# Where the y splits, one weight split and the last three p stand at the end of an attention

## The chip, the cores and the metric

The kernel runs on one core of a Trainium2 chip. The metric is device time in microseconds (us) of one execution. The core's engines run side by side, each through its own queue in program order: TensorE (PE in the profile; PEld are its weight loads), VectorE (DVE), ScalarE (ACT), GpSimd (POOL), and SyncE (SP), which here only issues DMAs. An instruction that waits holds up everything behind it on its engine.

## The reference, cut to what matters

One encoder layer for 1024 tokens and 1024 channels: a modulated RMS norm, one input projection, a pooling branch (512 channels) beside an attention with 8 heads (512 channels), an output projection and a gated residual.

```python
u_pool, g_pool, q_lat, kv_lat, k_rope_raw, g_attn = jnp.split(proj, offs, axis=-1)
y_pool = multiscale_pool(u_pool, pool_w[l], pool_scale[l]) * jax.nn.silu(g_pool)
...
s = jnp.einsum('bqhd,bkhd->bhqk', qblk, k, preferred_element_type=jnp.float32) * scale
p = jax.nn.softmax(s, axis=-1)
return jnp.einsum('bhqk,bkhd->bqhd', p.astype(v.dtype), v)
...
y = jnp.einsum('bsm,md->bsd', jnp.concatenate([y_pool, y_attn], axis=-1), w_out[l])
h = h + gate[:, None, :] * y
```

## The kernel before, in words

Products keep float32 accuracy by splitting each operand in two: a rounded **high half** and a **low half**, the rest (x minus high). Three matmuls, high·high, high·low and low·high, are summed. For the attention the halves are float16, for the projections a rounded float32.

**The attention** is a hand-written software pipeline (line 1005) over 64 jobs. Job i belongs to head i // 8 and step i % 8. Steps 0 to 3 (`hf` = 1) each take 128 query rows against all keys; steps 4 to 7 (`hf` = 0) each take 256 keys against the other 512 query rows. Tiles are named by head, `hf` and number: `st612` are the scores of head 6, `hf` 1, number 2, which is job 50; `st703` those of job 63. A job passes these stations:

- `scores`: six matmuls into a pair of PSUM banks (`st`). There are two such pairs in rotation; job 1 of each head (step 1) uses a third pair (tag `r`), which also holds the row maxima scores of `prep_max` and the transposed outputs `yt`. With `hf` = 1 DVE then takes the maximum over the row and scales it (L808, L809, tile `bp`).
- `expo` (ACT, L819): p = exp of the scores, into a tile `p` in SBUF, or in place, when `in_psum(i)` is true.
- `p_hi` (ACT, L824) and `p_lo` (L831): the two float16 halves of p (tile `ph`). `p_lo` runs on POOL, and on DVE for jobs whose p is in PSUM, which POOL doesn't read here. Before, those are steps 1 and 7 of a head, from job 7 on.
- `p_turn` (SP): with `hf` = 1 a DMA transposes `ph` to `pt`.
- `attend`: 16 matmuls into `av`, six jobs (LAG) behind `scores`; then `out_copy` (ACT L868, DVE L869) and `out_norm` (DVE L875, POOL L879) after the last job of a half head.

In steps 4 to 7 of head 6, `prep_max` takes the row maxima for four query blocks of head 7 (scores `rs70` to `rs73` on TensorE, maximum on DVE, L733). The maxima go into the first column of the tile `src1h` (the q source of the odd heads), and after the fourth a DMA transposes that column into q (L735).

**Work of the output projection that is put into the attention.** A table `extra`, filled by `at(head, step, ...)`, runs at the end of a step; steps 8 to 14 of head 7 are the seven in which the pipeline drains.

- `out_split` (L935 ACT, L937 POOL): the two halves of the output weights `oraw` of output tiles 0 and 1, in two pieces each, into `owhi` and `owlo`. For tile 1 these lie where `src1h` and its k counterpart were.
- `y_split` (L914 or L916 high half, L918 low half): the two halves of y0 to y6, the inputs of the output projection. y0 to y3 are the pooling outputs, y4 to y6 are heads 0 to 5, two heads each (tiles `gT0` to `gT2`; the last of them is ready after `out_tr` in step 4 of head 7). y7 (heads 6 and 7) follows behind the pipeline.
- `fill(0, k, k+1)`, steps 8 to 14: the six matmuls of y_k for output tile 0 (`ops`, L974). Behind the pipeline come tiles 1 to 7, 48 matmuls each.

What is on each engine in which order is thus set by the order of the calls within a step and by the two tables `XS`/`XS2` and `YP`.

Of the kernel before, what the change touches and what calls it, by code (L numbers as in the profile page):

```python
# [8 lines left out]
F32 = mybir.dt.float32  # L9
# [8 lines left out]
P = 128  # L18
# [3 lines left out]
H = 8  # L22
# [8 lines left out]
INV_2PI = 0.15915494309189535  # L31
INP = (1, 7)
XH = 6
XS = (4, 5)
XS2 = (2, 2)
YP = ((0, 4, 5, 1), (1, 6, 7, 1), (2, 8, 8, 1), (3, 9, 9, 0), (4, 10, 10, 0), (5, 11, 11, 0), (6, 12, 12, 0))
NF = 7
SG = 12
LAG = 6
# [19 lines left out]
def body(ctx, tc, small, cond, xT, ada_sc, ada_sh, ada_gt, w_lat, w_fm, pool_w, w_uq, w_ukv, gains, pos, w_out, out):  # L59
    nc = tc.nc  # L60
    V, A, G, T, SY = nc.vector, nc.scalar, nc.gpsimd, nc.tensor, nc.sync
# [146 lines left out]
    with ExitStack() as pa:  # L208
# [29 lines left out]
        for k in range(NK):  # L238
            pool, tag = (wp, "raw") if k in (0, 1, 6, 7) else (mp, wu_tags[k - 2])
# [462 lines left out]
    def conv_hi(h, w, eng, t0=0, t1=NK):  # L702
        o_, i_ = srcs[h % 2][w][:, 0, t0:t1, 1:HW], (QT, KT)[w][:, t0:t1, h, :]
        if eng is A:
            A.activation(o_, i_, AF.Copy)
        else:
            eng.tensor_copy(o_, i_)
# [40 lines left out]
    stp = ctx.enter_context(tc.tile_pool(name="psS", bufs=2, space=PSUM, reuse_waits="tile"))  # L748
    avp = ctx.enter_context(tc.tile_pool(name="psV", bufs=1, space=PSUM, reuse_waits="tile"))
    rsp = ctx.enter_context(tc.tile_pool(name="psR", bufs=1, space=PSUM, reuse_waits="tile"))  # L750
# [39 lines left out]
    def scores(i, n):  # L790
        h, hf, j = jobs[i]
        if n == 0:
            pool, tag = (rsp, "r") if h and hf and j == 1 else (stp, "st")
            stt[i] = pool.tile([P, 2, 512], F32, tag=tag, name=f"st{h}{hf}{j}")
        qh_, ql_ = qs[h]
        kh_, kl_ = ks[h]
        if hf == 0:
            kt = j * 2 + n
            for a, (l, r) in enumerate(((kh_, qh_), (kh_, ql_), (kl_, qh_))):
                T.matmul(stt[i][:, n], l[:HW, kt * P:(kt + 1) * P], r[:HW, 0:512], start=(a == 0), stop=(a == 2))  # L800
            return
        qt = 4 + j
        for a, (l, r) in enumerate(((qh_, kh_), (qh_, kl_), (ql_, kh_))):
            T.matmul(stt[i][:, n], l[:HW, qt * P:(qt + 1) * P], r[:HW, n * 512:(n + 1) * 512],  # L804
                     start=(a == 0), stop=(a == 2))
        if n:
            bps[i] = ep.tile([P, 1], F32, tag="bp", name=f"bp{h}{j}")
            V.tensor_reduce(bps[i], stt[i], AX.XY, ALU.max)  # L808
            V.tensor_scalar(bps[i], bps[i], nesc, 6.0 * LN2, ALU.mult, ALU.add)  # L809
# [15 lines left out]

    def in_psum(i):

        return i % 8 in INP and (i > 7 or i == 7)

    def p_lo(i):  # L830
        (V if in_psum(i) else G).tensor_tensor(pas[i][:, 1], pfs[i], pas[i][:, 0], ALU.subtract)  # L831
# [1 line left out]
    def p_turn(i):  # L833
        h, hf, j = jobs[i]
        if hf:
            pts[i] = a_tile("t", [P, 2 * NK, P], f"pt{h}{j}")
            SY.dma_start_transpose(pts[i], pas.pop(i).rearrange("p a n c -> p (a n c)"))
# [4 lines left out]
    def attend(i, n):  # L842
        h, hf, j = jobs[i]
        if j == 0 and n == 0:
            avt[0] = avp.tile([P, 2, 512], F32, tag="av", name=f"av{h}{hf}")

        def acc(qt, kt, hi, lo):
            o_ = avt[0][:, qt // 2, (qt % 2) * 256:(qt % 2) * 256 + 129]
            T.matmul(o_, hi, VT[:, kt, h, 0:129], start=kt == 0 and qt % 2 == 0, stop=False, skip_group_check=True)  # L849
            T.matmul(o_[:, 0:65], lo, VT[:, kt, h, 0:65], start=False, stop=kt == NK - 1, skip_group_check=True)  # L850

        if hf == 0:
            for qt in range(4):
                c_ = slice(qt * P, (qt + 1) * P)
                acc(qt, j * 2 + n, pas[i][:, 0, n, c_], pas[i][:, 1, n, c_])
            if n:
                pas.pop(i)
        else:
            for kt in range(4 * n, 4 * n + 4):
                acc(j, kt, pts[i][:, kt], pts[i][:, NK + kt])  # L860
# [3 lines left out]
    def out_copy(i):  # L864
        h, hf, _ = jobs[i]
        a4 = avt[0].rearrange("p b (i c) -> p (b i) c", i=2)
        ov = ovs[h, hf] = rb[:, hf * 512:hf * 512 + 260].rearrange("p (i c) -> p i c", i=4)
        A.activation(ov, a4[:, :, 64:129], AF.Copy)  # L868
        V.tensor_tensor(ov[:, :, 1:], a4[:, :, 0:64], ov[:, :, 1:], ALU.add)  # L869
# [14 lines left out]
    def out_tr(h, hfs, pt):  # L884
        for hf in hfs:
            for j in range(4):
                T.transpose(pt[:, hf, j * P:(j + 1) * P], opair[h // 2][:, hf, j, :], ident)
        c_ = slice(hfs[0] * 512, hfs[-1] * 512 + 512)
        pv = pt[:, hfs[0]:hfs[-1] + 1].rearrange("p b c -> p (b c)")
        if h < H - 1:  # L890
            V.scalar_tensor_tensor(gT[h // 2][:, c_], pv, vinv, gT[h // 2][:, c_], ALU.mult, ALU.mult)
        else:
            if not last:
                last.append(dp.tile([P, S], F32, tag="t0", name="ylast"))
            V.tensor_copy(last[0][:, c_], pv)
# [52 lines left out]
    def at(h, step, f, *a):  # L948
        extra.setdefault((h, step), []).append((f, a))
# [3 lines left out]
    for n in range(2):  # L953
        for part in range(2):
            for d in range(2):
                at(XH + d, XS[part] + XS2[d] * n, out_split, d, (n,), (part,), G)

    xr, ps = {}, {}

# [2 lines left out]
        SY.dma_start(xr[d], xT[d])  # L962

    def new(d):
        pool, tag = (stp, "st") if d % 3 < 2 else (rsp, "r")
        t_ = pool.tile([P, 2, 512], F32, tag=tag, name=f"ops{d}")
        ps[d] = [t_[:, 0], t_[:, 1]]

# [23 lines left out]
    at(7, 8, new, 0)  # L992
    for k in range(NF):
        at(7, 8 + k, fill, 0, k, k + 1)
    for k, s0, s1, e_ in YP:
        at(7, s0, y_split, k, (0, 1), (0,), (A, V)[e_])
        at(7, s1, y_split, k, (0, 1), (1,))

    def early(i, p_):

        for j in range(4):
            if RS0[j] == (i, p_):
                prep_max(0, j)

    for i in range(len(jobs) + LAG + 1):
        live = i < len(jobs)
        h, step = i // 8, i % 8
        a_ = i - LAG
        av_ok = 0 <= a_ < len(jobs)
        rh = h + (step > 3)  # L1010
        RSP = RSPY if rh in (4, 6, 8) else RSPN
        rsu = RSP.index(step) if live and 0 < rh < H and step in RSP else None
        e_ = i - 1 if 0 <= i - 1 < len(jobs) else None
        if 0 <= i - 3 < len(jobs):
            p_turn(i - 3)
        if av_ok and step in AF0:
            attend(a_, 0)
            attend(a_, 1)
            if jobs[a_][2] == 3:
                out_copy(a_)  # L1020
        early(i, 0)
        if live:
            scores(i, 0)
        early(i, 1)
        if live and h + 2 < H and step > 3:
            if step % 2 == 0:
                conv_hi(h + 2, 3 - step // 2, V)
            conv_lo(h + 2, 3 - step // 2, G, step % 2 * 4, step % 2 * 4 + 4)
        if live and 0 < h < H - 1 and step in TS:
            turn(h + 1, 1 - TS.index(step))  # L1030

        for hf in range(2):
            for n_ in (a_ - ON[hf],) if live else range(a_ - ON[hf], a_):
                if 0 <= n_ < len(jobs) and jobs[n_][1:] == (hf, 3) and jobs[n_][:2] in ovs:
                    out_norm(n_)
        if e_ is not None and jobs[e_][1] == 0:
            expo(e_)
        if 0 <= i - 2 < len(jobs):
            p_hi(i - 2)
            p_lo(i - 2)  # L1040
            pfs.pop(i - 2)
        if e_ is not None and jobs[e_][1]:
            expo(e_)
        if av_ok and step not in AF0 + AFL:
            attend(a_, 0)
        if NE + i < NK:
            last_fm(NE + i, NE + i + 1)
        if NE + i == NK - 1:
            last_end()
        early(i, 2)  # L1050
        if live:
            scores(i, 1)
        early(i, 3)
        if i == 3:
            fm_bias(11, lraw, rsp.tile([P, 2, 512], F32, tag="r", name="psb11")[:, 0])
        if av_ok and step in AFL:
            attend(a_, 0)
        if live and step == 4 and h in (3, 5, 7):
            out_tr(h - 2, (0, 1), rsp.tile([P, 2, 512], F32, tag="r", name=f"yt{h}"))
        if rsu is not None:  # L1060
            prep_max(rh, rsu)
        if av_ok and step not in AF0:
            attend(a_, 1)
            if jobs[a_][2] == 3:
                out_copy(a_)
        if i == 68:
            out_tr(H - 1, (1,), rsp.tile([P, 2, 512], F32, tag="r", name="yt8"))
        for f, a in extra.pop((min(h, H - 1), i - 8 * min(h, H - 1)), []):
            f(*a)
    assert not extra  # L1070
# [22 lines left out]
    for d in range(2, NK):  # L1093
# [15 lines left out]
        else:  # L1109
            for m, (a, b) in enumerate(LPARTS):  # L1110
                c_ = slice(a, b)
                pt = ps[d][0] if m == 0 else (rsp, avp)[m % 2].tile([P, 2, 512], F32, tag=("r", "av")[m % 2],
                                                                    name=f"opsl{m}")[:, 0]
# [80 lines left out]
```

## Time and profile before

| | |
|---|---|
| median of 3 runs | 501.46 us (501.36 to 502.86) |
| the execution profiled | 500.05 us, span of its trace 498.3 us |
| TensorE busy | 464.9 us, 93% of the span |
| DVE / ACT / POOL busy | 355.9 / 253.8 / 234.4 us |
| head 6, first scores of job 48 to those of job 56 | 354.18 to 374.79 us |
| head 7, from there to the scores of job 63 | 374.79 to 392.54 us |
| granted TensorE clock, mean of the span | 0.996 |

In the page's 40 slices of 12.5 us TensorE and its granted clock look like this (tenths, 9 is 90% or more); DVE and POOL beside them:

```profile
PE   5999998999999999999989888898898969999997
DVE  4888849999999853577677887877867985913221
POOL 1950040201242949448869796787869780000000
PEclk9999999999999999999999999999999999999999
```

The dip to 6 in slice 33 is the end of the attention (399 to 411 us). Timeline rows of the trace give the start from the span's start, the length, engine, line, operation and tiles, and in brackets how long the engine had been idle before and what ended that. Times are from one execution.

### The profile page before, as it was taken

The page shows a single profiled execution, that of the slowest core. Times are in us where ns is not written, and L with a number is a line of the kernel's source. Part 1 is how long each engine was busy: PE and PEld are TensorE (multiplying, and loading weights), DVE is VectorE, ACT ScalarE, POOL GpSimd, SP SyncE. Part 2 cuts the span into 40 slices and gives each one's busy share as a digit, 9 for nine tenths or more (in the row PEclk, how much of TensorE's full clock was granted, in tenths as well). Part 3 has the DMA queues.
Part 4 walks back from the last instruction along what each step waited for, and adds up shares of the span by engine and source line. Part 5 has one row for each costly group of instructions (what it writes and reads, how often), then busy time and mean ns, then how long its engine had stood idle before and what let it go on. Part 6 is the DMA issues. An engine that isn't in the chain of part 4 may idle for free.

```text
span 498.3 us, 7657 instructions
## 1 busy us (share of the span) xinstructions
PE 464.9 (93%) x2956; PEld 355.0 (71%) x2956; DVE 355.9 (71%) x565; ACT 253.8 (51%) x338; POOL 234.4 (47%) x190
## 2 busy tenths in 40 slices
PE   5999998999999999999989888898898969999997
PEld 3999876898888888785555555555555658888886
DVE  4888849999999853577677887877867985913221
ACT  3756038993203030226878888888899861001000
POOL 1950040201242949448869796787869780000000
PEclk9999999999999999999999999999999999999999
DMA  8894442000102110144786779779982836753333
GB/s 300 332 307 159 171 142 65 6 1 7 47 1 91 34 58 27 57 86 95 170 148 138 162 145 176 152 151 163 224 175 63 160 113 231 276 182 129 126 128 126
DMA packets 117046, 66.33 MB, mean 133 GB/s; under 512 B 105873, under 2 KB 107793, under 8 KB 117010
## 3 DMA queue, kind: packets, MB, share of 16 engines
q1 hardware_dynamic: 117010, 65.85, 49.9%
q8 instruction: 23, 0.38, 0.3%
q14 instruction: 13, 0.11, 0.1%
HBM read 35.43 MB, written 4.19 MB: 80 GB/s over the span
## 4 chain that ended last, share of the span: by engine, by line
PE 49%; DVE 22%; ACT 10%; POOL 10%; issue 5%; DMA 3%; SPq 0%; ACTq 0%; DVEq 0%; POOLq 0%
PE ops L974 14%; PE fps L170 8%; PE st L800 4%; PE pq L548 3%; ACT ph L824 3%; PE lps L234 3%; DVE bp L808 3%; POOL fraw L152 3%; ACT p L819 3%; DMA wlr<-in_w_lat 2%; PE rs L730 2%; PE av L849 2%; PE st L804 2%; POOL s L614 2%; DVE ph L831 2%
## 5 line engine op out<-in xcount | busy, mean ns | idle before, releaser
L831 POOL TENSOR_TENSOR ph<-p,ph 128x1024 f16<-128x1024 f32 x49 | 105.9, 2168 | 13.1 <-ACT ph L824 10.2
L170 PE MATMUL fps<-xh,whi 128*128 128x512 f32 x192 | 62.0, 404 | 0.5 <-ACT whi L147 0.5
L170 PE MATMUL fps<-xh,wlo 128*128 128x512 f32 x192 | 59.3, 390 | 0.1
L170 PE MATMUL fps<-xl,whi 128*128 128x512 f32 x192 | 59.3, 390 | 0.0
L800 PE MATMUL st<-q,k 97*128 97x512 f16 x192 | 49.5, 379 | 6.7 <-ACT p L819 6.6
L804 PE MATMUL st<-k,q 97*128 97x512 f16 x192 | 48.2, 379 | 8.0 <-ACT p L819 6.4
L824 ACT ACTIVATE ph<-p 128x1024 f16<-128x1024 f32 x49 | 51.7, 1055 | 0.5
L152 POOL TENSOR_TENSOR fraw<-fraw,shift 128x1024 f32<-128x1024 f32 x7 | 22.7, 3237 | 60.8 <-DVE wlo L148 53.8
L808 DVE TENSOR_REDUCE bp<-st 128x1 f32<-128x1024 f32 x32 | 39.0, 1220 | 5.2 <-PE st L804 3.4
L170 PEld LDWEIGHTS fps<-xh,whi 128*128 128x128 f32 x192 | 35.5, 189 | 9.0 <-ACT whi L147 1.0
L170 PEld LDWEIGHTS fps<-xh,wlo 128*128 128x128 f32 x192 | 36.0, 188 | 8.1 <-DVE wlo L148 0.5
L170 PEld LDWEIGHTS fps<-xl,whi 128*128 128x128 f32 x192 | 36.1, 188 | 7.7
L935 ACT ACTIVATE owhi<-oraw 128x1024 fp32r<-128x1024 f32 (+1 forms) x10 | 8.8, 885 | 54.0 <-DMA oraw<-in_w_out 54.0
L819 ACT ACTIVATE p<-st,bp,esc 128x1024 f32<-128x1024 f32 x25 | 30.1, 1204 | 9.4 <-DVE bp L809 9.0
L804 PEld LDWEIGHTS <-q 97*128 97x128 f16 x192 | 16.6, 97 | 25.6 <-issue 10.9
L800 PEld LDWEIGHTS <-k 97*128 97x128 f16 x192 | 16.6, 97 | 21.5 <-issue 8.3
L624 ACT ACTIVATE dh<-s 128x1024 fp32r<-128x1024 f32 x4 | 4.2, 1062 | 51.9 <-DVE s L621 51.9
L819 ACT ACTIVATE p<-st,ebias,esc 128x1024 f32<-128x1024 f32 x24 | 28.9, 1203 | 2.5 <-PE st L800 1.3
L850 PE MATMUL av<-VT,ph 128*128 128x65 f16 x256 | 26.4, 193 | 2.9 <-POOL ph L831 2.9
L849 PE MATMUL av<-VT,pt 128*128 128x129 f16 x256 | 28.0, 221 | 0.8 <-DMA pt<-ph 0.8
L849 PE MATMUL av<-VT,ph 128*128 128x129 f16 x256 | 27.7, 221 | 0.2 <-DVE rb L869 0.2
L850 PEld LDWEIGHTS <-ph 128*128 128x128 f16 x256 | 22.6, 98 | 7.1 <-POOL ph L831 3.1
(297 smaller groups left out, 1142.5 us busy)
## 6 DMA issues: line engine op xcount, KB each, us to landing
fraw<-in_w_fm SPq DMA_DIRECT2D x12, 512.0 KB, 3.7
asc<-in_ada_sc SPq DMA_DIRECT2D x8, 512.0 KB, 6.0
xr<-in_xT SPq DMA_DIRECT2D x8, 512.0 KB, 5.3
ash<-in_ada_sh SPq DMA_DIRECT2D x8, 512.0 KB, 6.8
oraw<-in_w_out SPq DMA_DIRECT2D x8, 512.0 KB, 5.1
xres<-in_xT SPq DMA_DIRECT2D x8, 512.0 KB, 5.0
agt<-in_ada_gt SPq DMA_DIRECT2D x8, 512.0 KB, 5.7
out_dram<-xres SPq DMA_DIRECT2D x7, 512.0 KB, 3.0
```

Of the source, the lines that this page charges most:

```text
L152: G.tensor_tensor(pb, pb, shift.unsqueeze(2).broadcast_to([P, NK, P]), ALU.mult)
L170: T.matmul(ps[n], w[:, k, :], x_[k][:, n * 512:(n + 1) * 512], start=(k == order[0] and j == 0), stop=(k == order[-1] and j == 2))
L234: T.matmul(ps[:, :LAT], l[k][:, ts_], r[k], start=(k == 0 and i == 0), stop=(k == NK - 1 and i == 2))
L800: T.matmul(stt[i][:, n], l[:HW, kt * P:(kt + 1) * P], r[:HW, 0:512], start=(a == 0), stop=(a == 2))
L804: T.matmul(stt[i][:, n], l[:HW, qt * P:(qt + 1) * P], r[:HW, n * 512:(n + 1) * 512], start=(a == 0), stop=(a == 2))
L808: V.tensor_reduce(bps[i], stt[i], AX.XY, ALU.max)
L819: A.activation(pfs[i], st, AF.Exp, bias=bps.pop(i) if hf else ebias, scale=esc)
L824: A.activation(pas[i][:, 0], pfs[i], AF.Copy)
L831: (V if in_psum(i) else G).tensor_tensor(pas[i][:, 1], pfs[i], pas[i][:, 0], ALU.subtract)
L849: T.matmul(o_, hi, VT[:, kt, h, 0:129], start=kt == 0 and qt % 2 == 0, stop=False, skip_group_check=True)
L850: T.matmul(o_[:, 0:65], lo, VT[:, kt, h, 0:65], start=False, stop=kt == NK - 1, skip_group_check=True)
L974: T.matmul(ps[d][n], w_[:, k, :], y_[k][:, n * 512:(n + 1) * 512], start=(k == 0 and j == 0), stop=(k == NK - 1 and j == 2))
```

## The change

Four tables or rules change. The y splits move from steps 4 to 12 of head 7 to head 6, step 1 to head 7, step 7, and all seven high halves are made by DVE (before, y3 to y6 by ACT). The split of output tile 1's weights moves from steps 4 to 7 of head 7 to its steps 0 to 3; that of tile 0 stays. The p of jobs 61 and 62 stays in PSUM beside that of job 63, and DVE, not POOL, makes their low halves. The PSUM tiles of the output projection rotate from another start: tile 0's sum takes the third pair, and `yt8`, the transposed output of head 7's second half, a pair of the scores.

```diff
-XS = (4, 5)
-XS2 = (2, 2)
-YP = ((0, 4, 5, 1), (1, 6, 7, 1), (2, 8, 8, 1), (3, 9, 9, 0), (4, 10, 10, 0), (5, 11, 11, 0), (6, 12, 12, 0))
+XS = (4, 0)
+YP = ((0, 6, 1, 2), (1, 6, 3, 4), (2, 6, 5, 6), (3, 7, 0, 1), (4, 7, 2, 3), (5, 7, 4, 5), (6, 7, 6, 7))
...
     def in_psum(i):
-        return i % 8 in INP and (i > 7 or i == 7)
+        return i % 8 in INP and i > 6 or i in (61, 62)
...
-                at(XH + d, XS[part] + XS2[d] * n, out_split, d, (n,), (part,), G)
+                at(XH + d, XS[d] + part + 2 * n, out_split, d, (n,), (part,), G)
...
-        pool, tag = (stp, "st") if d % 3 < 2 else (rsp, "r")
+        pool, tag = (stp, "st") if d % 3 else (rsp, "r")
...
-    for k, s0, s1, e_ in YP:
-        at(7, s0, y_split, k, (0, 1), (0,), (A, V)[e_])
-        at(7, s1, y_split, k, (0, 1), (1,))
+    for k, h_, s0, s1 in YP:
+        at(h_, s0, y_split, k, (0, 1), (0,), V)
+        at(h_, s1, y_split, k, (0, 1), (1,))
...
-            out_tr(H - 1, (1,), rsp.tile([P, 2, 512], F32, tag="r", name="yt8"))
+            out_tr(H - 1, (1,), stp.tile([P, 2, 512], F32, tag="st", name="yt8"))
```

**DVE in head 6**, from the maximum of job 49 (`bp61`) to that of job 51 (`bp63`) and on to the first row maximum for head 7 (`rs70`). Before:

```order
L808 TENSOR_REDUCE bp61_3797<-st611_3782 128x1
L808 TENSOR_REDUCE bp62_3811<-st612_3800 128x1
L875 RECIPROCAL rec51_3837<-rb_79 128x4
L831 TENSOR_TENSOR ph611_3840<-st611_3782,ph611_3840 128x1024
L808 TENSOR_REDUCE bp63_3856<-st613_3833 128x1
L733 TENSOR_REDUCE src1h_2045<-rs70_3889 128x1
```

Now:

```order
L808 TENSOR_REDUCE bp61_3797<-st611_3782 128x1
L916 CAST yq_3800<-yp0_801 128x1024
L808 TENSOR_REDUCE bp62_3814<-st612_3803 128x1
L918 TENSOR_TENSOR yq_3800<-yp0_801,yq_3800 128x1024
L875 RECIPROCAL rec51_3841<-rb_79 128x4
L831 TENSOR_TENSOR ph611_3844<-st611_3782,ph611_3844 128x1024
L808 TENSOR_REDUCE bp63_3860<-st613_3837 128x1
L916 CAST yq_3800<-yp1_1225 128x1024
L733 TENSOR_REDUCE src1h_2045<-rs70_3894 128x1
```

The scaling of each maximum (L809) stands right behind it and is not shown. y0's high half now stands ahead of job 50's maximum, its low half ahead of job 51's, and so on to y3 in head 7.

**ACT where head 7 begins**, from the high half of job 54 (`ph602`) to the exp of job 56 (`p710`). Before:

```order
L824 ACTIVATE ph602_4019<-p602_3984 128x1024
L868 ACTIVATE rb_79<-av61_3955 128x260
L824 ACTIVATE ph603_4066<-st603_3977 128x1024
L819 ACTIVATE p710_4069<-st710_4014,bp70_4025,esc_84 128x1024
L824 ACTIVATE ph710_4081<-p710_4069 128x1024
```

Now:

```order
L824 ACTIVATE ph602_4027<-p602_3992 128x1024
L935 ACTIVATE owhi1_4052<-oraw1_3689 128x512
L868 ACTIVATE rb_79<-av61_3962 128x260
L824 ACTIVATE ph603_4078<-st603_3985 128x1024
L819 ACTIVATE p710_4081<-st710_4022,bp70_4033,esc_84 128x1024
```

The first half of tile 1's high weights (`owhi1`) now stands three instructions ahead of the exp of job 56; before, it stood behind the exp of job 59. Its tile takes the place of `src1h`, so it comes after the DMA that transposes the row maxima out of it.

**DVE at the end of head 7**, from y4's low half to the low half of job 62 (`ph702`), now:

```order
L918 TENSOR_TENSOR yk_3801<-gT0_1848,yk_3801 128x1024
L891 SCALAR_TENSOR_TENSOR gT2_2021<-yt7_4185,vinv_82,gT2_2021 128x1024
L916 CAST yk_3801<-gT1_1931 128x1024
L869 TENSOR_TENSOR rb_79<-av60_4105,rb_79 128x4x64
L918 TENSOR_TENSOR yk_3801<-gT1_1931,yk_3801 128x1024
L916 CAST yh6_4267<-gT2_2021 128x1024
L875 RECIPROCAL rec60_4274<-rb_79 128x4
L831 TENSOR_TENSOR ph701_4278<-st701_4224,ph701_4278 128x1024
L918 TENSOR_TENSOR yl6_4268<-gT2_2021,yh6_4267 128x1024
L831 TENSOR_TENSOR ph702_4302<-st702_4239,ph702_4302 128x1024
```

The low halves of jobs 61 and 62 (`ph701`, `ph702`) were on POOL and are now here. Before, the list held y0 to y5 in this place, and of the low halves only job 63's. Job 63's scores (`st703`) go into the pair of PSUM banks that `st701` had; `ph701` is now the last reader of that pair, where it was job 61's exp.

## The prediction

> **What bounds the kernel now.** First the busy time by stretch, then TensorE's timeline through the end of the attention, to see which wait ends last there. Columns of a stretch: its length, then busy us (and instructions) of PE, PEld, DVE, ACT, POOL, the granted clock, DMA share, GB/s.
>
> ```profile
> 370.00:380.00 10.00, 8.99 (x93) 5.47 (x92) 6.51 (x8) 9.74 (x11) 9.04 (x6) 1.00 0.50 110
> 400.00:410.00 10.00, 6.20 (x65) 4.96 (x64) 8.69 (x6) 6.99 (x7) 9.16 (x5) 0.94 0.25 87
> 410.00:412.00 2.00, 2.00 (x7) 1.61 (x6) 1.63 (x2) 0.00 (x0) 0.00 (x0) 0.50 1.00 373
> ```
>
> In heads 6 and 7 ACT sets the pace (9.74 of 10 busy from 370 to 380); from 400 to 410 TensorE stands still for more than a third of the time. After 416 us TensorE runs without a wait, so the change can only move the moment at which it gets there. Its rows (start, length, what, and in brackets its idle time and who ended it):
>
> ```profile
> 392.54 0.81 PE L800 MATMUL st<-q,k 97*128 97x512 f16 x3
> 397.62 0.23 PE L849 MATMUL av<-VT,pt 128*128 128x129 f16 x1 [0.75 <-DMA pt<-ph]
> 400.11 0.22 PE L849 MATMUL av<-VT,ph 128*128 128x129 f16 x1 [0.16 <-DVE rb L869]
> 407.67 0.20 PE L850 MATMUL av<-VT,ph 128*128 128x65 f16 x1 [2.95 <-POOL ph L831]
> 409.22 1.12 PE L887 MATMUL yt<-ident,op 128*128 128x128 f32 x4 [0.74 <-POOL op L879]
> 409.99 2.06 PE L974 MATMUL ops<-yk,owhi 128*128 128x512 f32 x4
> 412.44 0.23 PE L849 MATMUL av<-VT,ph 128*128 128x129 f16 x1
> 413.15 1.18 PE L974 MATMUL ops<-yk,owhi 128*128 128x512 f32 x4
> 414.62 0.62 PE L974 MATMUL ops<-yh,owhi 128*128 128x512 f32 x2
> 415.99 0.60 PE L887 MATMUL ytl<-ident,op 128*128 128x128 f32 x4
> 416.34 1.18 PE L974 MATMUL ops<-yq,owhi 128*128 128x512 f32 x4
> ```
>
> The scores of job 63 begin at 392.54; the last early part of tile 0 ends at 415.99. In these 23.45 us TensorE is idle for 0.75 + 0.16 + 2.95 + 0.74 = 4.60. Behind the 2.95 us wait the clock is granted at 0.50 (row 410 to 412): six matmuls take 2.45 (409.99 to 412.44) where they later take 1.47 (413.15 to 414.62), four transposes 0.77 where they later take 0.35; 1.40 lost. That leaves **17.45 us of work**. The 6.0 us of idling and slow clock are all that can be won there; the 2.95 us wait is for POOL's low half of job 62.
>
> **What a moved instruction costs.** The y splits go to DVE, among the maxima of heads 6 and 7, while POOL makes low halves. How the two get on:
>
> ```profile
> 389.12 0.69 DVE L916 CAST yq<-yp 128x1024 fp32r<-128x1024 f32 x1
> 390.06 1.22 DVE L918 TENSOR_TENSOR yq<-yp,yq 128x1024 fp32r<-128x1024 f32 x1
> 391.47 2.41 POOL L831 TENSOR_TENSOR ph<-p,ph 128x1024 f16<-128x1024 f32 x1 [2.94 <-ACT ph L824]
> 391.91 3.04 DVE L918 TENSOR_TENSOR yq<-yp,yq 128x1024 fp32r<-128x1024 f32 x1
> 393.83 2.27 POOL L937 TENSOR_TENSOR owlo<-oraw,owhi 128x512 fp32r<-128x512 f32 x1
> 394.88 1.77 DVE L916 CAST yq<-yp 128x1024 fp32r<-128x1024 f32 x1
> 396.07 2.58 POOL L831 TENSOR_TENSOR ph<-p,ph 128x1024 f16<-128x1024 f32 x1
> L831 DVE TENSOR_TENSOR ph<-st,ph 128x1024 f16<-128x1024 f32 x2 | 2.5, 1225 | 1.2 <-ACT ph L824 1.2
> ```
>
> With POOL idle (until 391.47) a y cast takes 0.69 and a y low half 1.22; to the start of the next instruction 0.6 and 1.13, since rows overlap by some 0.09 (on ACT 391.28 and 392.37, below, are 1.09 apart for a length of 1.21). With POOL at work they take turns by whole instructions: the 3.04 us low half waits for POOL's instruction to end at 393.83 and ends 1.1 later; POOL's next, begun at 393.83, waits for that in turn (2.27); the cast of 394.88 waits until 396.07. A low half out of PSUM (last row, a group: two in head 6, mean 1225 ns, POOL busy) does not take part. So a moved y instruction costs its own time on DVE plus what is left of POOL's instruction, 0 to 2.1 us.
>
> **The sum, step by step.** Head 6 first:
>
> ```profile
> 361.24 2.14 POOL L831 TENSOR_TENSOR ph<-p,ph 128x1024 f16<-128x1024 f32 x1 [0.37 <-POOL src1h L716]
> 361.63 1.23 DVE L808 TENSOR_REDUCE bp<-st 128x1 f32<-128x1024 f32 x1
> 363.84 1.20 ACT L819 ACTIVATE p<-st,bp,esc 128x1024 f32<-128x1024 f32 x1
> 365.12 1.21 DVE L808 TENSOR_REDUCE bp<-st 128x1 f32<-128x1024 f32 x1
> 366.68 1.21 ACT L819 ACTIVATE p<-st,bp,esc 128x1024 f32<-128x1024 f32 x1 [0.55 <-DVE bp L809]
> 367.78 0.62 ACT L935 ACTIVATE owhi<-oraw 128x512 fp32r<-128x512 f32 x1
> 374.64 1.23 DVE L733 TENSOR_REDUCE src1h<-rs 128x1 f16<-128x1024 f32 x1 [1.12 <-PE rs L730]
> 375.90 1.19 SPq L735 DMA_TRANSPOSE q<-src1h  x1
> DMA to landing us min/median/max: 2.3/2.5/4.1
> 377.73 0.39 ACT L868 ACTIVATE rb<-av 128x260 f32<-128x260 f32 x1 [0.26 <-PE av L850]
> 378.02 1.02 ACT L824 ACTIVATE ph<-st 128x1024 f16<-128x1024 f32 x1
> 378.92 1.21 ACT L819 ACTIVATE p<-st,bp,esc 128x1024 f32<-128x1024 f32 x1
> ```
>
> 1. *Job 51.* The cast of y0 now stands where job 50's maximum began (361.63). POOL holds until 363.38, so the cast ends at 363.9. Job 50's maximum (1.4 with its scaling), y0's low half (1.13; POOL idles, waiting for a reciprocal behind it), the reciprocal and job 49's low half (1.25) put job 51's maximum at 367.7 instead of 365.12, its exp 1.56 later at 369.3 instead of 366.68: **+2.6**. ACT is full from here to the end of the head, so all of it stays.
> 2. *Job 56: a new wait.* Between 369.1 and head 7's last row maximum (rs73) DVE now also has two casts and two low halves: three maxima 3.4, casts 1.2, low halves 2.3, small ones 0.4, and 0.7 + 1.4 left of POOL's low halves of jobs 50 and 51: rs73 begins at 378.6 instead of 374.64. The transpose of those maxima goes out 1.26 later and lands 2.5 behind, at 382.3. The first quarter of tile 1's split, now in step 0 of head 7, writes the buffer which that transpose reads (`src1h`), and on ACT it stands ahead of job 55's high half and job 56's exp: 382.3 + 0.6 + 0.3 + 0.9 = 384.1 instead of 378.92: **+5.2**. Behind it wait DVE (job 55's low half) and TensorE (job 58's scores).
>
> ```profile
> 385.30 1.21 DVE L808 TENSOR_REDUCE bp<-st 128x1 f32<-128x1024 f32 x1
> 386.86 1.21 ACT L819 ACTIVATE p<-st,bp,esc 128x1024 f32<-128x1024 f32 x1 [0.61 <-DVE bp L809]
> 391.28 1.21 ACT L819 ACTIVATE p<-st,ebias,esc 128x1024 f32<-128x1024 f32 x1
> 392.37 1.06 ACT L824 ACTIVATE ph<-p 128x1024 f16<-128x1024 f32 x1
> 395.01 1.04 ACT L824 ACTIVATE ph<-p 128x1024 f16<-128x1024 f32 x1
> 395.96 1.17 ACT L819 ACTIVATE st<-st,ebias,esc 128x1024 f32<-128x1024 f32 x1
> ```
>
> 3. *Job 59.* From 384.4 DVE does job 55's low half, two maxima, y3's low half, y4's cast, a reciprocal and job 57's low half: 6.9, so job 59's maximum is at 391.3 or later instead of 385.30. Whether y4's cast gets ahead of POOL's low half of job 56 hangs on 0.2 us of my sum; if not, 1.9 more. Exp of job 59: +6.1 or +8.0.
> 4. *Job 61.* ACT gets back what steps 4 and 6 of head 7 are rid of (two splits of 0.6, of which I count 1.0, since it waits a little there now): exp at 396.4 or 398.3 instead of 391.28 (+5.1, +7.0).
> 5. *Job 63: the second new wait.* Its scores reuse the buffer in which p of job 61 now stays. Before, they needed job 61's exp alone (392.54 is 1.26 behind 391.28). Now ACT does that exp, job 60's high half, job 62's exp, job 61's high half (1.1, 0.95, 1.1; 1.12 until DVE can start) and DVE the low half (1.14): 5.4 instead of 1.26. DVE is later still: y4's low half, the gate multiply, both of y5 and the cast of y6 stand ahead, three of them behind POOL. Scores at **404.9** (406.3 at the other end of step 3) instead of 392.54.
> 6. *TensorE* has nothing else ahead of those scores, idles some 6 us and comes back to a slow clock, as in 410 to 412: 404.9 + 17.45 + 1.40 = 423.75 instead of 415.99: **+7.8** (+9.1). POOL's late low half of job 62, the old wait, is gone: DVE makes it before TensorE asks.
>
> By the Trainium skill, "TensorE: Matmul & The Clock Gate", section "HAM oscillation — how this bites in real kernels", an idle gap over about 3.4 us is followed by some 3.4 us at half rate. By it the loss would be 1.7 instead of the row's 1.4, and the sum +8.1; the 0.50 of 410 to 412 agrees.
>
> Priced at nothing: tile 0's sum moving to the third PSUM pair (free since step 4) and the later sums rotating with it (each reused two tiles, some 20 us, later; were that gone, an 0.7 us evacuation each). SP's order is unchanged; its transposes follow the low halves, which TensorE asks for later still.
>
> The execution profiled took 500.05 (span 498.3 and 1.75 around it), so 507.85; the median of the runs shown, 501.46, lies 1.4 above it, and on that scale it would be 509.3. I take the middle, a base of 500.75, here and for the rivals: **508.5**.
>
> **Rivals.**
> - *No turns to wait for (no change).* If each y instruction cost only its own time, job 51 is +0.9, rs73 no later than now, and only the transpose's landing (378.4) holds ACT: job 56 +1.3, job 59 +2.0, job 61 +1.0, scores of job 63 at 397.7, end at 397.7 + 17.45 + 1.40 = 416.5: +0.5, **501.3**. For it: POOL pauses in both heads. Against it: the 3.04 and 2.27 above, and POOL at 9.04 of 10.
> - *Half the turns.* The places drift, and half of DVE's waits fall into POOL's pauses: midway between +0.5 and +7.8, +4.1, **504.9**.
> - *Faster: the tail's wait goes, nothing replaces it.* Were job 61's exp no later than 391.28, job 63's scores begin at 396.7; with a wait under 3 us the clock stays: 396.7 + 17.45 = 414.1, −1.9, **498.9**. The place is ACT's queue at job 61's exp; it decides from there: up to 391.6 the kernel is faster by over 0.3%. For it: 2.13 on POOL become 1.22 on DVE. Against it: step 1 alone is past that point. The Trainium skill, "GPSIMD Engine Reference", section "4.1 Engine selection", sends two-input elementwise work to VectorE, GpSimd being about twice as slow; by that the move gains, and the two lengths agree.
> - *Worse.* Each turn lost, above **512**: the further end of step 3 and two turns of 2 us more.
>
> **How the numbers follow.** My sum, 506.5 to 512 by both ends of step 3 and the two scales, 0.64; half the turns, 503 to 506.5, 0.17; no change 0.09; faster 0.05; above 512 0.05. The range leaves out the last three, 0.19: **503 to 512**. About 0.3%, 1.5 us, is what a measurement of this kernel can tell from no change: faster 0.05, same 0.09, slower 0.64 + 0.17 + 0.05 = 0.86.
>
> **What will show it.** Job 50's maximum 2 us late behind a 2.3 us cast; ACT waiting for a DMA ahead of an `owhi` in step 0 of head 7; TensorE idle for several us before the `st` of job 63, released by DVE, then a clock near 0.5; no wait for POOL's `ph` in the tail. The prediction is wrong if y's casts take 0.7 throughout, if ACT doesn't wait at that split, or if job 63's scores begin before 399.

## The result, and the profile after

The changed kernel takes **509.54 us** (median of 4 runs, 509.35 to 510.26), the one before 501.41 (4 runs, 500.69 to 502.86): ratio 1.0167, 95% interval 1.0146 to 1.0188. The execution profiled took 509.35 with a span of 507.6; before, it was 500.05 and 498.3. Both differ by 9.3, and so does the end of tile 0's early part, 425.30 instead of 415.99. Behind that point the two traces run alike: 81.96 us from tile 1's first matmul to the end before, 81.95 now. The time is lost ahead of it. One execution of a run below, the one profiled of part A alone, took 593.64 us at a granted clock of 0.756; it is left out of every comparison, so that run has no places in the table.

The slices of the page of the changed kernel (12.7 us each) show where:

```profile
PE   5999998999999999999998988989796499999997
DVE  4888849999999682757787878877999934923231
POOL 1940030201434949447969779797669700000000
PEclk9999999999999999999999999999999979999999
```

DVE has four slices at 9 ahead of the end of the attention. TensorE falls to 6 and then 4, and behind that slice its clock dips to 7 (before, no slice was below 9).

DVE's and POOL's timeline in head 6 (rows as in the prediction):

```profile
360.93 2.13 POOL L831 TENSOR_TENSOR ph<-p,ph 128x1024 f16<-128x1024 f32 x1 [0.23 <-POOL src1h L716]
...
361.22 2.39 DVE L916 CAST yq<-yp 128x1024 fp32r<-128x1024 f32 x1
363.53 1.21 DVE L808 TENSOR_REDUCE bp<-st 128x1 f32<-128x1024 f32 x1
364.91 1.22 DVE L918 TENSOR_TENSOR yq<-yp,yq 128x1024 fp32r<-128x1024 f32 x1
...
367.24 1.22 DVE L808 TENSOR_REDUCE bp<-st 128x1 f32<-128x1024 f32 x1
```

The cast of y0 takes 2.39: POOL's low half ends at 363.06, the cast about 0.55 later. Job 50's maximum follows at 363.53 instead of 361.63, job 51's at 367.24 instead of 365.12.

ACT and SP's queue where head 7 begins, and ACT further on:

```profile
378.85 1.19 DVE L733 TENSOR_REDUCE src1h<-rs 128x1 f16<-128x1024 f32 x1
380.07 1.19 SPq L735 DMA_TRANSPOSE q<-src1h  x1
382.44 0.63 ACT L935 ACTIVATE owhi<-oraw 128x512 fp32r<-128x512 f32 x1 [2.04 <-DVE bp L809]
384.15 1.21 ACT L819 ACTIVATE p<-st,bp,esc 128x1024 f32<-128x1024 f32 x1
394.76 1.20 ACT L819 ACTIVATE p<-st,bp,esc 128x1024 f32<-128x1024 f32 x1 [2.67 <-DVE bp L809]
398.17 1.19 ACT L819 ACTIVATE st<-st,ebias,esc 128x1024 f32<-128x1024 f32 x1
```

The exps are those of jobs 56, 59 and 61 (before: 378.92, 386.86, 391.28). At `owhi` the trace names DVE's scaling as the releaser, but DVE had done that by 381.5. What fits 382.4 is the DMA of L735, which `owhi` must wait for: issued at 380.07, with landings of 2.3 to 4.3 us for this line in this trace.

DVE and TensorE at the end:

```profile
399.32 2.81 DVE L918 TENSOR_TENSOR yk<-gT,yk 128x1024 fp32r<-128x1024 f32 x1
402.05 2.60 DVE L916 CAST yh<-gT 128x1024 fp32r<-128x1024 f32 x1
404.66 1.19 DVE L831 TENSOR_TENSOR ph<-st,ph 128x1024 f16<-128x1024 f32 x1
405.90 1.44 PE L800 MATMUL st<-q,k 97*128 97x512 f16 x3 [5.60 <-DVE ph L831]
411.05 1.30 PE L974 MATMUL ops<-yq,owhi 128*128 128x512 f32 x4
425.30 0.60 PE L887 MATMUL ytl<-ident,op 128*128 128x128 f32 x4
```

The stretches around it (columns as in the prediction, the clock third from the end):

```profile
400.00:410.00 10.00, 4.40 (x34) 2.66 (x31) 6.98 (x5) 3.02 (x4) 4.72 (x3) 0.73 0.25 57
406.00:408.00 2.00, 2.00 (x12) 1.12 (x12) 0.98 (x1) 0.00 (x0) 0.00 (x0) 0.50 0.00 0
412.00:414.00 2.00, 2.00 (x23) 1.61 (x22) 0.69 (x1) 0.39 (x2) 0.00 (x0) 1.00 0.00 0
```

TensorE is busy 4.40 of the 10 us from 400. It waits 5.60 us for DVE's low half of job 61 (404.66), which stood on DVE behind two y instructions of 2.81 and 2.60. From 406 the clock is granted at 0.50, and only from 412 at 1.00. From the scores (405.90) TensorE works without a wait to 425.30: 19.40, which is 1.95 more than the prediction's 17.45 of work. The slow clock took more than these 1.95. From job 63's first scores to tile 0's first matmul the same instructions take 5.15 us now (405.90 to 411.05); before, they took 2.69, from 392.54 to this row:

```profile
395.23 1.18 PE L974 MATMUL ops<-yq,owhi 128*128 128x512 f32 x4
```

So 2.46 us went to the slow clock, and the work without any wait is nearer 16.9 us (19.40 less 2.46) than 17.45.

### The profile page after: what moved, and what is told of

Same layout as the page of the kernel before. It is cut to its first block, busy times and chain, and to the rows that moved or that the text cites. A ratio compares the mean times of both kernels' runs of the same rounds, so it can differ in the third digit from the quotient of the medians.

```text
span 507.6 us, 7654 instructions
## 1 busy us (share of the span) xinstructions
PE 467.3 (92%) x2956; PEld 355.3 (70%) x2956; DVE 364.0 (72%) x571; ACT 250.1 (49%) x334; POOL 228.9 (45%) x188
## 4 chain that ended last, share of the span: by engine, by line
PE 49%; DVE 24%; POOL 11%; ACT 8%; issue 5%; DMA 2%; SPq 0%; ACTq 0%; DVEq 0%; POOLq 0%
PE ops L974 15%; PE fps L170 8%; PE st L800 4%; PE pq L548 3%; POOL ph L831 3%; DVE bp L808 3%; POOL fraw L152 3%; PE av L849 3%; DMA wlr<-in_w_lat 2%; ACT ph L824 2%; PE rs L730 2%; PE lps L234 2%; POOL s L614 2%; PE pk L558 2%; ACT p L819 2%
## 5 line engine op out<-in xcount | busy, mean ns | idle before, releaser
L831 POOL TENSOR_TENSOR ph<-p,ph 128x1024 f16<-128x1024 f32 x47 | 102.4, 2184 | 10.7 <-ACT ph L824 8.0
L800 PE MATMUL st<-q,k 97*128 97x512 f16 x192 | 51.4, 390 | 14.8 <-ACT p L819 9.1
L824 ACT ACTIVATE ph<-p 128x1024 f16<-128x1024 f32 x47 | 49.6, 1055 | 0.5
L800 PEld LDWEIGHTS <-k 97*128 97x128 f16 x192 | 16.9, 99 | 30.2 <-issue 17.1
L831 DVE TENSOR_TENSOR ph<-st,ph 128x1024 f16<-128x1024 f32 x17 | 20.7, 1219 | 11.9 <-ACT ph L824 11.3
L850 PE MATMUL av<-VT,pt 128*128 128x65 f16 x256 | 27.7, 197 | 0.0
L819 ACT ACTIVATE p<-st,ebias,esc 128x1024 f32<-128x1024 f32 x22 | 26.5, 1203 | 2.5 <-PE st L800 1.3
```

Of the source, the lines that this page charges most:

```text
L819: A.activation(pfs[i], st, AF.Exp, bias=bps.pop(i) if hf else ebias, scale=esc)
L824: A.activation(pas[i][:, 0], pfs[i], AF.Copy)
```

## The experiments

Call the three parts **A** (y's splits), **B** (tile 1's weight split) and **C** (p of jobs 61 and 62 in PSUM, with the rotation of the PSUM tiles). The question is which of them costs the 8 us, and whether it is the turns with POOL. Each ratio is to the kernel before on the same chip. "Left" is the stretch from job 63's scores to the end of tile 0's early part less the 17.45 of work, that is, waits and slow clock; since the work is some 0.5 less, each is that much too low. "Maximum of 49" is the start of job 49's maximum on DVE, which stands ahead of every edit: what differs there is one execution against another and belongs to no part.

| run | parts | us | ratio (95%) | maximum of 49 | exp of 61 | scores of 63 | end of early part | left |
|---|---|---|---|---|---|---|---|---|
| before | none | 501.41 | 1 | 360.15 | 391.28 | 392.54 | 415.99 | 6.00 |
| after | A B C | 509.54 | 1.0167 (1.0146 to 1.0188) | 359.84 | 398.17 | 405.90 | 425.30 | 1.95 |
| e1_y_only | A | 504.18 | 1.0061 (1.0040 to 1.0083) | | | | | |
| e2_xs_only | B | 497.61 | 0.9927 (0.9900 to 0.9954) | 361.24 | 395.57 | 396.82 | 415.58 | 1.31 |
| e3_psum_only | C | 501.11 | 1.0010 (0.9998 to 1.0022) | 359.54 | 391.12 | 397.16 | 416.72 | 2.11 |
| e4_no_psum | A B | 501.74 | 1.0022 (1.0011 to 1.0034) | 359.62 | 399.61 | 401.18 | 418.54 | -0.09 |
| e5_no_xs | A C | 509.92 | 1.0173 (1.0144 to 1.0201) | 360.10 | 400.26 | 406.30 | 425.37 | 1.62 |
| e6_no_y | B C | 501.72 | 1.0025 (1.0003 to 1.0046) | 361.94 | 396.23 | 401.75 | 421.28 | 2.08 |
| e9_only62 | A B, p of 62 alone | 502.74 | 1.0036 (1.0017 to 1.0055) | 359.86 | 398.13 | 400.10 | 417.92 | 0.37 |

The executions profiled of e2 and e6 took 499.64 and 505.35, more than their medians, so their places are up to 2 and 3.6 us late. For A alone, e7 below has the same order up to step 4 of head 7.

**One part alone, and one part undone.** The edits are the lines of the change, each part either as before or as after: `YP` and the loop that reads it are A, `XS` and its `at` line B, `in_psum` with the two lines on `pool` and `yt8` C. C alone on the kernel before, for one:

```diff
-        return i % 8 in INP and (i > 7 or i == 7)
+        return i % 8 in INP and i > 6 or i in (61, 62)
...
-        pool, tag = (stp, "st") if d % 3 < 2 else (rsp, "r")
+        pool, tag = (stp, "st") if d % 3 else (rsp, "r")
...
-            out_tr(H - 1, (1,), rsp.tile([P, 2, 512], F32, tag="r", name="yt8"))
+            out_tr(H - 1, (1,), stp.tile([P, 2, 512], F32, tag="st", name="yt8"))
```

> The kernel before with one part of the change: y's splits in their new slots on DVE; tile 1's split and the PSUM buffers as before. Theory (turns with POOL, then the two new waits): job 51 late by 2.6 as in the changed kernel, job 61's exp at about 395.8 instead of 391.28; job 63's scores follow it at once, TensorE's early part of tile 0 ends 0.5 to 4.5 later than 415.99, 502 to 506 us, 504 the likeliest. Rival 1 (the moved instructions cost only their own time on DVE, the loss comes from the PSUM wait): 501.4 or less. Rival 2 (the transpose wait at tile 1's split carries the loss): 501.4.

> The kernel before with tile 1's weight split in steps 0 to 3 of head 7, nothing else. Theory: the maxima's transpose lands at 378.4 as before, so ACT loses 1.3 at job 56, gets it back in steps 4 and 6; POOL is rid of two low halves of 1.7 to 2.3 in the tail, so the 2.95 wait for POOL's low half of job 62 shrinks: 498.5 to 501, 499.5 the likeliest. Rival 2 (this wait carries most of the loss): 506 or more.

> The kernel before with p of jobs 61 and 62 kept in PSUM and the rotation of the PSUM pairs that goes with it, nothing else. Theory: job 61's exp stays at 391.28, job 63's scores begin 5.4 to 7.2 behind it (396.7 to 398.5) instead of 1.26, the wait for POOL's low half of job 62 is gone: end of tile 0's early part 0.5 earlier to 1.4 later, 501 to 503 us, 501.7 the likeliest. Rival 1 (the PSUM wait is the loss by itself): 507 or more.

> The changed kernel with p of jobs 61 and 62 and the PSUM pairs as before: both other parts stay. Theory: the chain up to job 61's exp as in the changed kernel (398.2), job 63's scores 1.3 behind it, then waits for POOL's low halves of 2 to 4 us: 504.4 to 507.9, 506 the likeliest. Rival 1 (the PSUM wait is the loss): 501.4 or less.

A alone costs 3.5 us, as the theory of turns has it. B alone wins 3, more than the 498.5 to 501 expected; e10 below, which moves its split past the wait, wins no more (0.9925 beside 0.9927). C alone is no change, as expected: job 63's scores wait, and the old waits are gone. ACT and TensorE of that run (C alone):

```profile
391.12 1.18 ACT L819 ACTIVATE st<-st,ebias,esc 128x1024 f32<-128x1024 f32 x1
397.16 1.44 PE L800 MATMUL st<-q,k 97*128 97x512 f16 x3 [4.67 <-DVE ph L831]
416.72 0.60 PE L887 MATMUL ytl<-ident,op 128*128 128x128 f32 x4
```

The expectation of e4 failed: 501.7 where the theory said 504.4 to 507.9. Job 61's exp is later still than the 398.2 expected (from 387 to 392 the clock is granted at 0.50, behind a wait of 2.73), but the waits that I expected behind job 63's scores are not there (A and B, without C):

```profile
399.61 1.21 ACT L819 ACTIVATE p<-st,ebias,esc 128x1024 f32<-128x1024 f32 x1
401.18 0.81 PE L800 MATMUL st<-q,k 97*128 97x512 f16 x3
405.89 0.23 PE L849 MATMUL av<-VT,pt 128*128 128x129 f16 x1 [0.37 <-DMA pt<-ph]
418.54 0.60 PE L887 MATMUL ytl<-ident,op 128*128 128x128 f32 x4
```

From the scores to the end are 17.36, 0.37 of it a wait: next to nothing is left to win there. With y's splits out of the tail and tile 1's low halves off POOL, POOL makes its low halves in time. So A and B together are 8.6 late at job 63's scores (401.18 for 392.54) and get 6.1 of it back behind them, and the wait that C takes off POOL is gone without C.

> The changed kernel with tile 1's split in its old steps; y's splits and the PSUM buffers as changed. Theory (the second wait is dear only when job 61's exp is late): job 61's exp at about 395.8, job 63's scores 5.4 to 7.7 behind it, then 17.45 of work and the slow clock: 504.5 to 507, 506 the likeliest. Rival 3 (the parts simply add up): 504.2 of the y splits alone plus 0.4 of the PSUM buffers alone, 504.6. Rival 2 (the wait at tile 1's split carries the loss): 502 or less.

> The changed kernel with y's splits in their old slots (four casts on ACT); tile 1's split and the PSUM buffers as changed. Theory of the prediction (y's turns make everything late): no turns ahead of job 61, 500 to 503 us, 501.4 the likeliest. Theory as the last runs leave it (any lateness of job 61's exp makes the second wait dear; tile 1's split alone makes it 4 late): scores of job 63 at 401 to 402.5, 504 to 506. Rival 3 (the parts add up): 498.

Both speak against parts that simply add up (504.6 and 498 by that rival, 509.9 and 501.7 measured). e6's median came out as the prediction's own theory had it. Its execution profiled, the slowest (505.35), has job 63's scores at 401.75, as the other theory had it, so the median doesn't show that this theory's account of the places is right. e5 is 3 us above the theory's range, since job 61's exp is 9.0 late (400.26) and not the 4.5 that I had counted. Adding C costs 0.1% alone, and 1.0 to 1.45% where A, B or both stand already (1.0061 to 1.0173, 0.9927 to 1.0025, 1.0022 to 1.0167): its price is the same wait behind job 61's exp each time (5.5 to 7.7 us from that exp to job 63's scores), but only alone does it still take the old waits away with it. And e5 speaks on the wait at tile 1's split: without it the kernel is no faster (1.0173 beside 1.0167). Its trace, ACT and TensorE (A and C, without B):

```profile
391.30 1.44 PE L800 MATMUL st<-q,k 97*128 97x512 f16 x3 [3.05 <-ACT p L819]
393.76 1.20 ACT L819 ACTIVATE p<-st,bp,esc 128x1024 f32<-128x1024 f32 x1 [1.43 <-DVE bp L809]
400.26 1.18 ACT L819 ACTIVATE st<-st,ebias,esc 128x1024 f32<-128x1024 f32 x1
406.30 1.44 PE L800 MATMUL st<-q,k 97*128 97x512 f16 x3 [4.68 <-DVE ph L831]
```

Job 59's exp is 1.0 earlier than in the changed kernel (394.76), job 61's 2.1 later (398.17): TensorE, granted 0.50 from 391 to 396 behind its 3.05 us wait, and the split that stands in step 5 again take back what the missing wait gives. So B's move is no net loss; what its wait costs by itself this run doesn't separate.

**Turns, or DVE's own time?** Two kernels add fourteen DVE instructions to the kernel before, in the changed kernel's slots: once the splits themselves, so that each is made twice, and once maxima of the same length with one input.

```diff
+    def extra_op(k, part):
+        y_split(k, (0, 1), (part,), V)
...
+    for k, h_, s0, s1 in ((0, 6, 1, 2), (1, 6, 3, 4), (2, 6, 5, 6), (3, 7, 0, 1), (4, 7, 2, 3), (5, 7, 4, 5), (6, 7, 6, 7)):
+        at(h_, s0, extra_op, k, 0)
+        at(h_, s1, extra_op, k, 1)
```

In the second kernel `extra_op` is a maximum instead:

```diff
-        y_split(k, (0, 1), (part,), V)
+        V.tensor_reduce(ep.tile([P, 1], F32, tag="xm", name=f"xm{k}{part}"), (yp + gT)[k][:, 0:512 + 512 * part],
+                        AX.X, ALU.max)
```

> The kernel before with y's casts and low halves done twice: in the changed kernel's slots on DVE, and again where they were. Theory of turns: the added casts in heads 6 and 7 take 1.5 to 2.6 where POOL is busy, job 51's maximum 2.6 late, the tail with its old waits: 503.5 to 507, 505 the likeliest. Rival 1 (own time only): casts of 0.7, 501 to 502.5.

> As the run before, but in place of each added cast a maximum over 512 columns of the same y tile (0.6 us alone), and in place of each added low half a maximum over its 1024 columns (1.2 us alone): the same time on DVE with one input, and no result is used. Theory of turns: these wait for no POOL instruction, 0.6 and 1.2 throughout, job 51's maximum about 0.9 late, 501 to 502.5 us. Rival 1 (own time only): the same as the run before within 0.7 us. Rival 4 (any DVE instruction on SBUF takes turns): as the run before, with maxima of 1.5 to 3.

The first takes 512.98 us, ratio 1.0253 (1.0214 to 1.0292), the second 502.77, ratio 1.0042 (1.0024 to 1.0061). DVE's groups from 360 to 396 us (count, busy us, mean ns), of the kernel with splits and then of the one with maxima:

```profile
L916 DVE CAST yq<-yp 128x1024 fp32r<-128x1024 f32 x3 | 6.4, 2119 | 0.0
L916 DVE CAST yk<-yp 128x1024 fp32r<-128x1024 f32 x1 | 2.6, 2608 | 0.0
```

```profile
L921 DVE TENSOR_REDUCE xm<-yp 128x1 f32<-128x512 f32 x4 | 2.7, 676 | 0.0
L921 DVE TENSOR_REDUCE xm<-yp 128x1 f32<-128x1024 f32 x4 | 4.8, 1209 | 0.0
```

And ACT's exp of job 61 in the first and in the second:

```profile
401.03 1.21 ACT L819 ACTIVATE p<-st,ebias,esc 128x1024 f32<-128x1024 f32 x1
```

```profile
393.73 1.21 ACT L819 ACTIVATE p<-st,ebias,esc 128x1024 f32<-128x1024 f32 x1
```

The same slots and the same own time: the maxima take 676 and 1209 ns throughout, the casts 2119 and 2608 on average. The two executions are apart already at job 49's maximum, ahead of every added instruction (360.56 and 361.63; before, 360.15). Counted from there, the splits make job 61's exp 9.34 late and the maxima 0.97. **The turns, with what follows from them, are 8.4 us of it**; a wait of 3.05 us on TensorE with a slow clock behind it (at 391.80) is among what follows. The rival by which every DVE instruction on SBUF takes turns is out too. I had the size too small (503.5 to 507 expected for the splits). Besides job 61's exp, the tail of that kernel, which still has its own splits, takes 25.49 us from job 63's scores to the end of tile 0's early part, and the kernel before 23.45.

**Which buffer.** The changed kernel, with job 61's p back in SBUF:

```diff
-        return i % 8 in INP and i > 6 or i in (61, 62)
+        return i % 8 in INP and i > 6 or i == 62
```

> The changed kernel, but p of job 61 goes to SBUF again; p of job 62 stays in PSUM, and so does the changed rotation of the pairs. Theory (the one dear wait is that of job 63's scores for the low half out of job 61's pair): exp of job 61 at 398 to 399.6, scores of job 63 at 1.3 to 1.6 behind it instead of 7.7, no slow clock: 500.5 to 503 us, 501.5 the likeliest. Rival 5 (the new rotation, or job 62's p in PSUM, is what costs): 507 or more.

502.74 us. ACT and TensorE of that kernel:

```profile
398.13 1.21 ACT L819 ACTIVATE p<-st,ebias,esc 128x1024 f32<-128x1024 f32 x1
400.10 0.81 PE L800 MATMUL st<-q,k 97*128 97x512 f16 x3
417.92 0.60 PE L887 MATMUL ytl<-ident,op 128*128 128x128 f32 x4
```

Job 61's exp stands where the changed kernel has it (398.17), job 63's scores 5.80 earlier and the early part's end 7.38. One buffer held for one low half is some 6.6 of the 8.1 us (1.0167 less 1.0036); the rotation and job 62's p are not.

**A version that beats both.** B gained in spite of its place. Moved one step on, past the transpose of the maxima:

```diff
-XS = (4, 5)
-XS2 = (2, 2)
+XS = (4, 1)
...
+                at(XH + d, XS[d] + part + 2 * n, out_split, d, (n,), (part,), G)
```

> The kernel before with tile 1's split in steps 1 to 4 of head 7 instead of 5 to 8: past the transpose of the maxima, and POOL still rid of two low halves in the tail. Theory: no wait at job 56, job 61's exp at 391.3 to 392.5, 1.4 to 2 of waits behind job 63's scores instead of 4.60: 496 to 498.5 us, 497 the likeliest. Rival 6 (an early split costs head 7 its 4 us wherever it stands, as in steps 0 to 3): 497.6 as that run, with job 61's exp at 395. Rival 7 (POOL's low half of job 62 still waits for DVE's y splits): 500 to 501.

> The run before, with p of job 62 alone kept in PSUM (and the rotation of the pairs that this needs), so that DVE and not POOL makes its low half. Theory: what is left of the wait for POOL's low half of job 62 goes: 0 to 1.4 us less than the run before, 495.5 to 498. Rival (that low half now stands on DVE behind y's splits, which wait for POOL): the same or up to 1 us slower than the run before.

497.24 us, ratio 0.9925 (0.9896 to 0.9954), no more than B in its first place (0.9927); and with job 62's p in PSUM besides (`or i == 62`, with C's rotation) 498.07, ratio 0.9940 (0.9919 to 0.9961): nothing more. Of the first, TensorE's waits in the tail and DVE's row behind the second:

```profile
398.04 0.23 PE L849 MATMUL av<-VT,pt 128*128 128x129 f16 x1 [0.81 <-DMA pt<-ph]
398.98 3.05 DVE L918 TENSOR_TENSOR yq<-yp,yq 128x1024 fp32r<-128x1024 f32 x1
402.42 0.22 PE L849 MATMUL av<-VT,ph 128*128 128x129 f16 x1 [2.03 <-DVE rb L869]
412.87 0.60 PE L887 MATMUL ytl<-ident,op 128*128 128x128 f32 x4
```

The wait for POOL is gone; what is left is a turn, a y low half of 3.05 ahead of L869. So one y split alone was moved to where POOL is idle in head 6:

```diff
-YP = ((0, 4, 5, 1), (1, 6, 7, 1), (2, 8, 8, 1), (3, 9, 9, 0), (4, 10, 10, 0), (5, 11, 11, 0), (6, 12, 12, 0))
+YP = ((0, 4, 4, 1), (1, 12, 13, 1), (2, 14, 15, 1), (3, 17, 17, 0), (4, 18, 18, 0), (5, 19, 19, 0), (6, 20, 20, 0))
...
-        at(7, s0, y_split, k, (0, 1), (0,), (A, V)[e_])
-        at(7, s1, y_split, k, (0, 1), (1,))
+        at(6 + (s0 > 7), s0 - 8 * (s0 > 7), y_split, k, (0, 1), (0,), (A, V)[e_])
+        at(6 + (s1 > 7), s1 - 8 * (s1 > 7), y_split, k, (0, 1), (1,))
```

Steps count from head 6 here: y0 stands in its step 4, y1 in steps 4 and 5 of head 7, y2 in its steps 6 and 7, the others where they were.

> The kernel before with tile 1's split in steps 1 to 4 of head 7, and y0's split alone (cast and low half on DVE) in step 4 of head 6, where POOL idles for 2.5 us (368.4 to 370.95 in the run with tile 1's split alone); y1 and y2 move one place up in head 7. Theory (a split costs only its own time where POOL idles, and the tail loses one turn): cast of y0 0.7, low half 1.2, the 2.03 us in which TensorE waits in the tail for DVE's L869 behind y2's low half shrinks: 495 to 496.7 us, 496 the likeliest. Rival 8 (the 1.7 us by which L869 of head 6 moves back holds TensorE and ACT, which is full there): 497.2 to 499.

**495.66 us**, ratio 0.9894 (0.9880 to 0.9908). Its DVE in head 6, then job 61's exp and TensorE:

```profile
369.85 0.68 DVE L916 CAST yq<-yp 128x1024 fp32r<-128x1024 f32 x1
370.56 1.22 DVE L918 TENSOR_TENSOR yq<-yp,yq 128x1024 fp32r<-128x1024 f32 x1
...
393.29 1.21 ACT L819 ACTIVATE p<-st,ebias,esc 128x1024 f32<-128x1024 f32 x1
412.76 0.60 PE L887 MATMUL ytl<-ident,op 128*128 128x128 f32 x4
```

No turn in y0's split, as expected. The rival is right too, for a small part. Job 61's exp is 1.87 later than in e10 (391.42), but 1.29 of that stands already at job 50's maximum (362.92 beside 361.62), ahead of the moved split: 0.6 is the split's. Against it stands the 2.03 wait, which is gone. In the two executions profiled the early part ends within 0.11 of each other, and the two intervals overlap; that both beat the kernel before is shown, that the second beats the first is not.

## Why the prediction was right, and where it was off

Its slower kernel and its mechanism were right; 508.5 was predicted and 509.54 measured.

1. *Job 51.* Predicted +2.6: maximum at 367.7, exp at 369.3. Measured 367.24 and 368.80. Turns are the cause, shown by the pair of added splits and added maxima: counted from job 49's maximum, job 51's is 2.43 late with the splits, as in the changed kernel, and 0.70 with the maxima.
2. *Job 56, the new wait.* Predicted 384.1, measured 384.15, with `rs73` at 378.85 where 378.6 was predicted; the landing of the transpose fits the end of the wait. The wait is real, but the moved split is **no net term of the loss**: with it in its old steps the time is the same (1.0173 beside 1.0167). The sum carried the wait on to job 59, where in e5 DVE's queue is nearly as late without it (393.76). No run has the changed kernel with the split past the transpose, so what this wait costs there by itself stays open.
3. *Job 59.* Predicted 393.0 or 394.9, measured 394.76: POOL's low half of job 56 did get ahead of y4's cast. The tie went to the further end.
4. *Job 61.* Predicted 396.4 or 398.3, measured 398.17.
5. *Job 63's scores.* Predicted 404.9 or 406.3, measured 405.90. That this wait, for the pair of job 61, decides is shown by e9.
6. *TensorE.* Predicted 423.75 (+7.8), measured 425.30 (+9.3). Of the 1.55 between them 1.00 is the later start of the scores (405.90 for 404.9, towards the further end of step 3). The other 0.55 is what is left of two terms that were off and partly cancel: **the slow clock, taken as 1.40, took 2.46**, by the same instructions as above, and **the 17.45 of work is nearer 16.9** (e4, with a single wait of 0.37 and no slow clock there, has 17.36 less 0.37, 16.99). That the sum came nearer than its terms is luck. The step also credits the new placing with the end of POOL's old wait; e4 shows that this wait goes with A and B, without C.

Of the rivals, "no turns" falls with e8: maxima without turns cost 2.2 us. "Faster" had the kernel faster with job 61's exp no later than 391.6. C alone speaks against it: the exp stands at 391.12, and the time is the same (1.0010). Job 63's scores come 6.04 behind that exp, not 5.4, after a wait of 4.67 and not under 3, and the clock doesn't stay; behind the 2.95 us wait of the kernel before it didn't either. e10 holds the exp at 391.42 and is faster, but by taking work off POOL in the tail and with no p moved. Priced at nothing, the rotation of the PSUM tiles and SP's order showed no wait.

What stays open: how much of A's 3.5 us its tail gives back, since A's chain was read only in its twin, e7, and when a short wait is followed by a slow clock. The executions of B alone (496.60 to 499.64) and of B with C (501.18 to 505.35) spread with the granted clock: B alone took 496.60 and 496.70 at a mean of 1.000, 498.52 at 0.993 and 499.64 at 0.990, and the two slowest with C had 0.985 and 0.982, the lowest of their ten. In the slowest of B alone, the one profiled, the clock is at 0.50 from 384 to 388, behind a wait of 2.06; so its job 61 is later than the median's is likely to be.

## What to carry to other kernels

A wait at the end of a phase can be a reserve that pays for lateness ahead of it: count what each part of a change takes from it, since two parts that remove the same waits win them only once, and the second still costs its own price. Before work is moved to an engine with idle time, look at what its neighbour does in that very slot: here one split in a pause of POOL took 0.68 and 1.22, and in the changed kernel, beside POOL's work, splits took up to 2.61 and 2.81. And when a result is kept in the buffer it was computed in, add to its saving the wait of the next one who needs that buffer, counted from the end of the queue of the engine that now frees it. And before places of two traces are compared, look at a point ahead of every edit: here the executions stood up to 2.4 us apart there (359.54 to 361.94).

## What the runs showed of the hardware

- A DVE maximum over one float32 tile in SBUF takes no turns with POOL (676 and 1209 ns beside POOL's low halves), while a float32 cast of the same tile does (2119 on average beside POOL's work; 0.68 us with POOL idle, where the maximum takes 1.21). The Trainium skill, "SBUF — State Buffer", section "SBUF: two separate sides", has a port pair that DVE and GpSimd hold for whole instructions, on DVE's side for those with two inputs in SBUF or in a fast two-port mode. The trace agrees on all three kinds.
- The length of a wait alone doesn't tell whether TensorE's clock slows behind it. Six score matmuls behind a short wait in B alone, in A and B, and in e9:

```profile
382.32 2.72 PE L804 MATMUL st<-k,q 97*128 97x512 f16 x6 [2.06 <-ACT p L819]
386.45 2.72 PE L804 MATMUL st<-k,q 97*128 97x512 f16 x6 [2.73 <-ACT p L819]
385.37 1.46 PE L804 MATMUL st<-k,q 97*128 97x512 f16 x6 [2.73 <-ACT p L819]
```

  Behind the same 2.73 us they run at half speed in A and B and at full speed in e9, where the clock is at 0.50 only from 387 on. What decides isn't shown.
- Nor does the loss grow with a longer wait. From job 63's scores to tile 0's first matmul, 2.69 us at full clock, it takes 5.00 behind a wait of 4.16 (e6), 5.15 behind 4.67 (e3), 4.90 behind 4.68 (e5) and 5.15 behind 5.60 (the changed kernel): 2.2 to 2.5 lost each time. The Trainium skill, "TensorE: Matmul & The Clock Gate", section "HAM oscillation — how this bites in real kernels", speaks of gaps above some 3.4 us, and by it the prediction had a loss of 1.7; here shorter gaps do it too, and the measurement decides.
